# The second parts of the odd attention's queries in tiles of 128 rows, half of them zero

## The chip, the cores and the metric

The kernel runs on one core of one Trainium2 chip. The metric is the device time of one execution in microseconds; the figure of a kernel is the median of its runs. Engines: PE multiplies matrices (PEld is its weight load), DVE, ACT and POOL work on tiles, SP issues most DMAs.

## The reference, cut to what matters

A two-layer encoder runs over a prompt of 512 tokens and a sample of 256 tokens with the same weights, all in float32. Each layer is feed-forward, mixer, feed-forward. The mixer of the second (odd) layer, and the only one that the change touches, is windowed attention with 16 query heads and 4 key heads of 64 features, in blocks of 128 tokens:

```python
s = jnp.einsum('bqgrd,bkgd->bgrqk', q_n, k_n).astype(f32) * scale + bias[None]
s = jnp.where(valid, s, NEG_INF)
m = jnp.maximum(jnp.max(s, axis=-1, keepdims=True), sk)
p = jnp.exp(s - m)
denom = jnp.sum(p, axis=-1, keepdims=True) + jnp.exp(sk - m)
return jnp.einsum('bgrqk,bkgd->bqgrd', (p / denom).astype(v.dtype), v_n)
```

`q_n` holds 128 queries, `k_n` up to 384 keys (the block before, the own block and the block after, as far as the sequence has them).

## The kernel before, in words

Float32 products are made of float32r products: a number x is split into a rounded first part and a second part x - first part, and three of the four products of parts are summed in PSUM. The weights come as tiles `raw`, are split by ACT (first part, L88) and DVE (second part, L89) into tiles `whl`, and are used in a fixed order. `self.look` says how many tiles of weights are prepared ahead. PSUM is a ring of eight banks (`self.ps()`), `raw` a ring of seven tiles.

The six stages run one after the other: ffn 0, `mixer0`, ffn 1, ffn 2, `mixer1`, ffn 3. `mixer1` makes the keys (`keys`, in `kk`), the values (`V`, L1009) and the queries `qT[0]` (`block`, L222), and then weaves two attention passes with dense products: `att(0)` with the four feature blocks of `qT[1]` (L222, emptied by ACT at L893), `att(1)` with half of the output projection (`out_pass`, L389, added to x by DVE at L392). `weave` emits one step of the dense product and then two steps of the attention; the compiler that orders each engine's instructions keeps this nearly as it is, but may mix neighbouring steps.

A pass `att(m)` has 12 units u: six query tiles (order 4, 5, 0, 1, 2, 3) by two key heads (`par`). `queries(t)` splits the queries of a tile: `hh` has the first part of a key head's four query heads twice, above each other (ACT at L927 and L930, POOL at L932), and `lo` has the second parts, par 0 in rows 0 to 63 and par 1 in rows 64 to 127 (DVE, L928). `kk` holds for each key head its first part in the 64 rows that its queries have, and its second part in the other 64. So `scores(u)` needs two matmuls for each of four heads: L956 over all 128 rows gives first part by first part plus first part of the query by second part of the key, and L957, over 64 rows, adds the second part of the query by the first part of the key. DVE adds the bias and takes the maximum (L958), ACT makes the exponentials with their sum (L960), DVE and ACT make the divisor (L962 to L965), DVE scales (L968). `values(u)` transposes the four heads' rows on PE (L978), ACT copies them from PSUM (L981, one copy for each key tile), and for par 1 PE multiplies with the values, 64 output rows for each key head (L990). Then ACT stores (L1017 in `att(0)`, the split at L88 and L89 in `att(1)`).

The order in a step of the weave is: dense step, `values(u)`, `scores(u+2)`, so that a unit's transposes come one dense step, one `values` and one `scores` and another dense step behind its scores. A unit has 256 keys for query tiles 4, 5, 0 and 3, and 384 for tiles 1 and 2.

Of the kernel before, what the change touches and what calls it, by code (L numbers as in the profile page):

```python
# [11 lines left out]
F32 = mybir.dt.float32  # L12
F32R = mybir.dt.float32r
# [6 lines left out]
P = 128  # L20
# [17 lines left out]
# neighbourhood attention: (first query, queries, first key, keys) in the order (column, row)  # L38
NA_Q = [(0, 128, 0, 256), (128, 128, 64, 256), (256, 128, 192, 256), (384, 128, 256, 256),
        (512, 128, 512, 160), (640, 128, 608, 160)]  # L40
# key blocks (first key, keys) of the windows above
# [5 lines left out]
class Trunk:  # L47
# [20 lines left out]
    def warm(self, after):  # L68
        """have the table of the square root loaded as soon as the column "after" is there"""
        w = self.cp.tile([P, 1], F32, tag="warm", name="warm", bufs=2)  # L70
        self.nc.scalar.activation(w, after, AF.Sqrt, bias=self.one, scale=0.0)
# [13 lines left out]
    def split(self, hl, lo, src):  # L85
        """hl (rounded) + lo = src, exactly"""
        nc = self.nc
        nc.scalar.copy(hl, src)  # L88
        nc.vector.tensor_sub(lo, src, hl.bitcast(F32))  # L89

# [6 lines left out]
    def weights(self):  # L97
        """the weights of the whole trunk"""
# [15 lines left out]
        def quad(n, q, b, r1=None):  # L114
            """the parts and sums of two blocks of features; without the head if r1, the first, is given"""
            k = lambda z: (n, q, b, z)
            headed, r1 = r1 is not None, self.raw(self.a[n][q, 2 * b]) if r1 is None else r1
            a11, a12 = r1[:, :512], r1[:, 512:]
            if not headed:
                yield k("11"), self.part(a11)  # L120
            r2 = self.raw(self.a[n][q, 2 * b + 1])
            a21, a22 = r2[:, :512], r2[:, 512:]
            s1 = self.wp.tile([P, 512], F32, tag="st", name="st", bufs=2)
            v.tensor_add(s1, a21, a22)  # L124
            v.tensor_sub(a21, a11, a21)
            v.tensor_sub(a11, s1, a11)
            yield k("s2"), self.part(a11)
            yield k("s1"), self.part(s1)
            if b < 2:
                yield k("22"), self.part(a22)  # L130
            yield k("s3"), self.part(a21)
            if not headed:
                yield k("12"), self.part(a12)
            v.tensor_sub(a12, a12, a11)
            yield k("s4"), self.part(a12)
            if b > 1:
                yield k("22"), self.part(a22)
# [57 lines left out]
    def norm_half(self, t, out):  # L195
        """sum of squares of the first half of token tile t"""
        ss = self.cp.tile([P, 4], F32, tag="ss", name="ss", bufs=6)
        self.nc.scalar.activation(out[:, 0:512], self.x[t][:, 0:512], AF.Square, accum_out=ss[:, 0:1])  # L198
        self.nc.gpsimd.tensor_scalar(ss[:, 1:2], ss[:, 0:1], 1.0 / DM, EPS, ALU.mult, ALU.add)  # L199
        return ss  # L200

    def norm_rows(self, t, gb, out, ss, parts=1):
        """out = rms_norm of token tile t"""
        nc = self.nc
        nc.scalar.activation(out[:, 512:1024], self.x[t][:, 512:1024], AF.Square, accum_out=ss[:, 2:3])
        nc.scalar.activation(ss[:, 3:4], ss[:, 2:3], AF.Sqrt, bias=ss[:, 1:2], scale=1.0 / DM)
        nc.vector.reciprocal(ss[:, 0:1], ss[:, 3:4])
        for e in range(parts):
            c = slice(e * DM // parts, (e + 1) * DM // parts)
            nc.vector.scalar_tensor_tensor(out[:, c], self.x[t][:, c], ss[:, 0:1], gb[:, c], ALU.mult, ALU.mult)  # L210
# [7 lines left out]
    def gemm(self, o, w, act, k0, n, kk=range(KM), last=KM - 1):  # L218
        """o[128 features, n tokens] = w^T act, w stationary; w and act hold four blocks of 128 features to a tile"""
        for k in kk:  # L220
            for j, i in ((0, 0), (0, 1), (1, 0)):
                self.nc.tensor.matmul(o, w[k // 4][:, j, k % 4 * P : (k % 4 + 1) * P], act[i][k // 4][:, k % 4, k0 : k0 + n],  # L222
                                      start=k == 0 and (j, i) == (0, 0), stop=k == last and (j, i) == (1, 0))

    def ffn(self, q, norm, tail, extra=None):
        """gate and up by Winograd's form of Strassen's product over 2 blocks of features, of inputs and of tokens"""
        nc = self.nc
# [3 lines left out]
        with ExitStack() as ctx:  # L231
# [18 lines left out]
            def quad(n, b, use):  # L250
                """steps of the four blocks; use(feature block, token half, value)"""
# [97 lines left out]
    def rows(self, hs, q, b, pos, tail=None):  # L349
        """steps of x += 0.5 h wd over a pair of blocks of features"""  # L350
# [22 lines left out]
    def out_pass(self, name, kb, half, act, tail=None):  # L373
        """steps of x[:, half] += act w over k-block kb (4 of 128 features); act(part, k) has all tokens"""
# [24 lines left out]
    def fgemm(self, f, hn, evac, norm=None, kk=KM):  # L399
        """steps of a feature block of act @ w, feature-major; f names the weights, evac(psum, first token, tokens)"""  # L400
        st = {}

        def part(n, k0, m, ks):
            if not st:
                st["w"] = [self.take(*z) for z in f]
            if ks[0] == 0:
                st["o"] = self.ps()[:, 0:m]
            self.gemm(st["o"], st["w"], hn, k0, m, ks, kk - 1)
            if ks[-1] == kk - 1:
                evac(st["o"], k0, m)  # L410
            if n == 0 and norm:
                norm.finish()

        h = kk // 2
        return [lambda: part(0, NP, NS, range(kk)), lambda: part(1, 0, NP, range(h)), lambda: part(2, 0, NP, range(h, kk))]

# [1 line left out]
    def s5_matrices(self, pool, spare):  # L418
# [10 lines left out]
        class Room:  # L429
            """carves blocks out of tiles"""  # L430
# [26 lines left out]
        def exp(out, x):  # L457
            """exp to float32's accuracy"""
# [51 lines left out]
        # (a - 1) / lambda  # L510
# [15 lines left out]
        # powers 0..8  # L526
# [40 lines left out]
        def start(q):  # L567
            """a pair of groups: W2 (state -> outputs), W1 (inputs -> state)"""
# [28 lines left out]
        def finish(q):  # L597
            """W1 transposed, E (inputs -> outputs)"""
# [44 lines left out]
    def mixer0(self, norm, tail):  # L643
# [4 lines left out]
        with ExitStack() as ctx:  # L648
            mp = ctx.enter_context(self.tc.tile_pool(name="mix0", bufs=1))

            # inputs of S5, in (chunk position, channel) rows
# [14 lines left out]
            def qkv(h):  # L666
                """steps of a head pair's values, queries and keys, in the order (column, row)"""
# [28 lines left out]
            def na(h):  # L696
                """steps of a head pair; q is overwritten by the output, feature-major"""
# [65 lines left out]
            # chunk inputs of the states; both directions run from slot to slot, the reversed one backwards in time  # L763
# [31 lines left out]
            # outputs of S5: chunk inputs through M, states before the chunk through W2  # L795
# [54 lines left out]
            # the neighbourhood half of the output projection around the gate of S5  # L850
# [25 lines left out]
    def mixer1(self, norm, tail):  # L876
        nc, a = self.nc, self.a
        hn = norm.hn
        with ExitStack() as ctx:
# [4 lines left out]
            # a key head's two parts above each other, the first part in the rows that its queries have  # L884
            kk = self.big([P, 4, NT], F32R, name="kk")
            V = mp.tile([P, 6, 256], F32, name="V", tag="V")
            halves = slice(0, 64), slice(64, P)
            pt6, turn = self.big([P, 6, 512], name="pt"), [0]
# [7 lines left out]
            # (query tile, first key tile, key tiles, first column of the bias)  # L896
# [20 lines left out]
            def att(m, store):  # L917
                """steps of the heads of key heads 2m and 2m+1"""
                bias, pend, pts, qq = [] if m else [bias0], {}, [], {}

                def queries(t):
                    """the first parts twice above each other, and the second parts"""
                    q = qT[m][:, :, t * P : (t + 1) * P]
                    hh = self.wp.tile([P, 2, 512], F32R, tag="whl", name="whl", bufs=8).rearrange("p e (h n) -> p e h n", h=4)
                    lo = mp.tile([P, 4, P], F32R, tag="ql", name="ql", bufs=2)
                    for e, r in enumerate(halves):
                        nc.scalar.copy(hh[r, e], q[r])  # L927
                        nc.vector.tensor_sub(lo[r], q[r], hh[r, e].bitcast(F32))  # L928
# [6 lines left out]
                def scores(u):  # L935
# [11 lines left out]
                    r = slice(par * 64, par * 64 + 64)  # L947
                    ps = []
                    hh = (2 * m + par) * 4
                    for h2 in range(2):  # L950
                        p = self.raw()[:, : 2 * 384].rearrange("p (e n) -> p e n", e=2)
                        for e in range(2):
# [4 lines left out]
                            nc.tensor.matmul(s[:, :n], ql[r, h], z[r], start=False, stop=True)  # L957
# [111 lines left out]
def weave(main, *sides):  # L1069
    """emit the steps of main with those of the sides spread between them"""  # L1070
# [13 lines left out]
class NormOut:  # L1084
    """final rms_norm, a token tile at a time"""
# [17 lines left out]
class NormT:  # L1103
    """rms_norm, transposed to feature-major in two parts, a token tile at a time"""
# [41 lines left out]
class NormS(NormT):  # L1146
    """the same as the sums that ffn multiplies with; tokens of tiles 4, 5, 0 and of 1, 2, 3 face each other"""
# [46 lines left out]
    def rest(self):  # L1194
        """the parts that later products take, a step for each"""
# [39 lines left out]
def _na_index(t):  # L1235
    """row of the padded table for each (query, key) of query tile t"""
# [9 lines left out]
def _layout(i):  # L1246
# [13 lines left out]
    # heads of the odd layer: tile (m, r) holds head r of key heads 2m and 2m+1  # L1260
# [5 lines left out]
    # S5  # L1266
# [11 lines left out]
    # biases by constant index; the last entry of the padded table is the masked one  # L1278
# [26 lines left out]
```

## Time and profile before

| | us |
|---|---|
| median of three runs | 2751.83 |
| fastest and slowest run | 2750.31, 2754.99 |
| span of the profiled execution | 2751.6 |
| PE busy in it | 2695.9 (98%) |
| DVE busy | 2008.4 (73%) |
| ACT busy | 1176.3 (43%) |
| POOL busy | 340.6 |

The profiled execution lies within 0.3 us of the median. A matmul's shown duration has a modelled end, and matmuls overlap, so what one costs is read from the distance between the starts of neighbours and not from its duration. A group of weight loads has a count and a total, and where the total is less than count times the single load, loads overlap. In the tables of stretches each engine's field is its busy time in the stretch, PEclk is the granted clock of PE as a share of 2.4 GHz (0.50 is 1.2 GHz).

### The profile page before, as it was taken

The page shows a single profiled execution, that of the slowest core. Times are in us where ns is not written, and L with a number is a line of the kernel's source. Part 1 is how long each engine was busy: PE and PEld are TensorE (multiplying, and loading weights), DVE is VectorE, ACT ScalarE, POOL GpSimd, SP SyncE. Part 2 cuts the span into 40 slices and gives each one's busy share as a digit, 9 for nine tenths or more (in the row PEclk, how much of TensorE's full clock was granted, in tenths as well). Part 3 has the DMA queues.
Part 4 walks back from the last instruction along what each step waited for, and adds up shares of the span by engine and source line. Part 5 has one row for each costly group of instructions (what it writes and reads, how often), then busy time and mean ns, then how long its engine had stood idle before and what let it go on. Part 6 is the DMA issues. An engine that isn't in the chain of part 4 may idle for free.

```text
span 2751.6 us, 38966 instructions
## 1 busy us (share of the span) xinstructions
PE 2695.9 (98%) x14636; PEld 2422.3 (88%) x14636; DVE 2008.4 (73%) x3878; ACT 1176.3 (43%) x2464; POOL 340.6 (12%) x688
## 2 busy tenths in 40 slices
PE   7999999998999999999999999999999999999998
PEld 7988988888888999999989999999876689999997
DVE  8967776772964887677789776767557678777776
ACT  6333333343565633333354333334457664333333
POOL 0156654300840000000000000000000000000000
PEclk9999999999999999999999999999999999999999
DMA  4122222316244222121203121211201123122221
GB/s 155 65 90 85 90 90 77 127 54 134 89 125 142 81 81 85 54 85 54 88 29 122 62 77 62 79 61 39 100 16 39 45 72 108 63 76 68 71 70 54
DMA packets 81245, 217.48 MB, mean 79 GB/s; under 512 B 22848, under 2 KB 29632, under 8 KB 80800
## 3 DMA queue, kind: packets, MB, share of 16 engines
q1 hardware_dynamic: 77152, 203.91, 23.4%
q0 software_dynamic: 3904, 11.08, 1.2%
q8 instruction: 115, 1.88, 0.3%
q14 instruction: 74, 0.61, 0.1%
HBM read 199.17 MB, written 17.89 MB: 79 GB/s over the span
## 4 chain that ended last, share of the span: by engine, by line
PE 92%; DVE 3%; DMA 2%; ACT 2%; POOL 1%; issue 1%; SPq 0%; DVEq 0%; ACTq 0%; POOLq 0%
PE ps L247 44%; PE ps L362 25%; PE ps L222 8%; PE ps L389 5%; PE ps L957 1%; PE ps L990 1%; PE ps L956 1%; PE ps L978 1%; PE ps L1133 1%; PE ps L1009 1%; PE ps L774 1%; PE ps L616 1%; DVE raw L210 1%; PE ps L746 1%; DVE whl L89 0%
## 5 line engine op out<-in xcount | busy, mean ns | idle before, releaser
L88 ACT CAST whl<-raw 128x512 fp32r<-128x512 f32 x796 | 480.3, 621 | 943.7 <-PE ps L362 446.6
L247 PE MATMUL ps<-bt,whl 128*128 128x384 f32 x4224 | 764.6, 336 | 8.9 <-DVE ct L273 8.9
L247 PEld LDWEIGHTS ps<-bt,whl 128*128 128x128 f32 x4224 | 737.9, 189 | 12.5 <-DVE ct L273 10.1
L362 PE MATMUL ps<-whl,hl 128*128 128x512 f32 x3168 | 732.7, 391 | 0.0
L89 DVE TENSOR_TENSOR whl<-raw,whl 128x512 fp32r<-128x512 f32 x796 | 550.6, 705 | 220.2 <-ACT whl L88 209.2
L362 PEld LDWEIGHTS ps<-whl,hl 128*128 128x128 f32 x3168 | 593.9, 188 | 123.5 <-ACT hl L88 0.9
L247 PE MATMUL ps<-b,whl 128*128 128x384 f32 x3168 | 580.3, 336 | 0.0
L247 PEld LDWEIGHTS ps<-b,whl 128*128 128x128 f32 x3168 | 555.1, 189 | 3.5 <-ACT hct L617 0.3
L365 DVE SCALAR_TENSOR_TENSOR x<-ps,x 128x512 f32<-128x512 f32 x528 | 361.5, 689 | 217.5 <-PE ps L362 215.3
L199 POOL TENSOR_SCALAR ss<-ss 128x1 f32<-128x1 f32 x42 | 11.3, 270 | 1787.2 <-ACT raw L198 1787.2
L222 PE MATMUL ps<-hn,whl 128*128 128x256 f32 (+1 forms) x1248 | 231.2, 342 | 1.4 <-ACT hn L88 1.4
L222 PEld LDWEIGHTS ps<-hn,whl 128*128 128x128 f32 x1248 | 191.8, 190 | 31.8 <-issue 3.3
L88 ACT CAST hl<-hct 128x384 fp32r<-128x384 f32 x176 | 86.9, 512 | 50.8 <-DVE hct L317 44.9
L389 PE MATMUL ps<-whl,ob 128*128 128x512 f32 x432 | 105.2, 399 | 0.0
L89 DVE TENSOR_TENSOR hl<-hct,hl 128x384 fp32r<-128x384 f32 x176 | 98.3, 577 | 7.7 <-ACT hl L88 7.4
L389 PEld LDWEIGHTS ps<-whl,ob 128*128 128x128 f32 x432 | 80.7, 190 | 19.7 <-issue 2.2
L279 ACT COPY ct<-ps 128x384 f32<-128x384 f32 x88 | 42.3, 481 | 102.4 <-PE ps L247 102.4
L314 ACT ACTIVATE hct<-ct 128x384 f32<-128x384 f32 x88 | 46.3, 526 | 91.3 <-DVE ct L285 79.9
L284 DVE TENSOR_TENSOR ct<-ps,hct 128x384 f32<-128x384 f32 x88 | 48.9, 556 | 29.3 <-PE ps L247 29.1
L124 DVE TENSOR_TENSOR st<-raw 128x512 f32<-128x512 f32 x88 | 62.6, 712 | 10.1 <-DMA raw<-in_w_gate 9.2
L958 DVE CUSTOM_DVE_ANT_0 raw<-ps,gb,sk 128x256 f32<-128x256 f32 (+1 forms) x96 | 48.6, 525 | 29.0 <-PE ps L957 25.8
L392 DVE TENSOR_TENSOR x<-ps,x 128x512 f32<-128x512 f32 x48 | 33.0, 688 | 48.6 <-PE ps L389 48.6
(235 smaller groups left out, 2632.8 us busy)
## 6 DMA issues: line engine op xcount, KB each, us to landing
raw<-in_w_gate SPq DMA_DIRECT2D x92, 512.0 KB, 3.6
raw<-in_w_up SPq DMA_DIRECT2D x92, 512.0 KB, 3.6
raw<-in_w_down SPq DMA_DIRECT2D x88, 512.0 KB, 3.7
raw<-in_w_in_even SPq DMA_DIRECT2D x16, 512.0 KB, 3.6
raw<-in_w_in_odd SPq DMA_DIRECT2D x10, 512.0 KB, 4.8
W2d<-raw POOLq DMA_DIRECT2D x16, 256.0 KB, 2.4
W1d<-hct POOLq DMA_DIRECT2D x16, 256.0 KB, 3.0
raw<-W1d SPq DMA_DIRECT2D x8, 512.0 KB, 5.5
```

The costliest lines, as they stand in the source:

```text
L88: nc.scalar.copy(hl, src)
L89: nc.vector.tensor_sub(lo, src, hl.bitcast(F32))
L124: v.tensor_add(s1, a21, a22)
L222: self.nc.tensor.matmul(o, w[k // 4][:, j, k % 4 * P : (k % 4 + 1) * P], act[i][k // 4][:, k % 4, k0 : k0 + n], start=k == 0 and (j, i) == ...
L247: nc.tensor.matmul(o, w[:, j, k * P : (k + 1) * P], B[z][:, i, k], start=first and k == 0 and (j, i) == (0, 0), stop=k == 3 and (j, i) == ...
L279: nc.scalar.copy(bank["r5"], bank[3])
L284: v.tensor_add(u3, bank[2], bank["p1"])
L314: nc.scalar.activation(at(f, t), o, AF.Silu)
L362: nc.tensor.matmul(o, h[i][:, pos[t] * P : (pos[t] + 1) * P], w[half][:, j], start=n == 0 and (j, i) == (0, 0), stop=n == len(hs) - 1 and ...
L365: nc.vector.scalar_tensor_tensor(xs, o, 0.5, xs, ALU.mult, ALU.add)
L389: nc.tensor.matmul(o, act(i, k)[:, t * P : (t + 1) * P], st["w"][k][:, j], start=m == 0, stop=m == 11)
L958: nc.vector.tensor_tensor_reduce(p[:, e, :n], s[:, :n], bias[0][:, par * 4 + h, c0 : c0 + n], -1.0, sk[:, 1, hh + h : hh + h + 1], ALU.add ...
```

## The change

The tile `lo` of a query tile, one of two rotating buffers [128, 4, 128], becomes one of two tiles `second[i]` [128, 2, 4, 128] that live as long as `mixer1`. POOL fills both with zeros once at the start of `mixer1`. DVE writes the second parts of key head par to rows `halves[par]` of slot par; the other 64 rows of the slot stay zero. L957 then takes the whole slot and the whole key tile in place of 64 rows of each. The tiles need 4 KB more of each partition, and the reservation for POOL's DMA descriptors is set to 8192 bytes. The full diff also removes comments and docstrings, which moves no line but those below the added ones; they are left out.

```diff
             V = mp.tile([P, 6, 256], F32, name="V", tag="V")
             halves = slice(0, 64), slice(64, P)
+            second = [mp.tile([P, 2, 4, P], F32R, tag=f"ql{i}", name="ql") for i in range(2)]
+            for z in second:
+                nc.gpsimd.memset(z.bitcast(F32), 0.0)
             pt6, turn = self.big([P, 6, 512], name="pt"), [0]
...
-                    lo = mp.tile([P, 4, P], F32R, tag="ql", name="ql", bufs=2)
+                    lo = second[len(qq) % 2]
                     for e, r in enumerate(halves):
                         nc.scalar.copy(hh[r, e], q[r])
-                        nc.vector.tensor_sub(lo[r], q[r], hh[r, e].bitcast(F32))
+                        nc.vector.tensor_sub(lo[r, e], q[r], hh[r, e].bitcast(F32))
...
-                    r = slice(par * 64, par * 64 + 64)
...
                             nc.tensor.matmul(s[:, :n], qh[:, par, h], z, start=True, stop=False)
-                            nc.tensor.matmul(s[:, :n], ql[r, h], z[r], start=False, stop=True)
+                            nc.tensor.matmul(s[:, :n], ql[:, par, h], z, start=False, stop=True)
...
-    nc = _bacc.Bacc("TRN2", target_bir_lowering=False, num_devices=1)
+    nc = _bacc.Bacc("TRN2", target_bir_lowering=False, num_devices=1, dynamic_dma_scratch_size=8192)
```

## Rows read from the trace of the kernel before

**Rows 1.** The page: busy time by engine, share of the span and instructions.
```profile
PE 2695.9 (98%) x14636; PEld 2422.3 (88%) x14636; DVE 2008.4 (73%) x3878; ACT 1176.3 (43%) x2464; POOL 340.6 (12%) x688
```

**Rows 2.** Instructions of PE in order, both passes: start, us, line, operation, shape, count.
```profile
2012.24 0.28 PE L956 MATMUL ps<-kk,whl 128*128 128x256 f32 x1
...
2047.68 0.38 PE L956 MATMUL ps<-kk,whl 128*128 128x256 f32 x1
2047.99 0.38 PE L957 MATMUL ps<-kk,ql 64*128 64x256 f32 x1
...
2050.18 3.06 PE L222 MATMUL ps<-hn,whl 128*128 128x512 f32 x12
...
2053.87 0.42 PE L956 MATMUL ps<-kk,whl 128*128 128x384 f32 x1
...
2056.80 3.14 PE L222 MATMUL ps<-hn,whl 128*128 128x256 f32 x24
2059.77 1.04 PE L978 MATMUL ps<-ident,raw 128*128 128x128 f32 x8
...
2109.59 0.28 PE L956 MATMUL ps<-kk,whl 128*128 128x256 f32 x1
```

**Rows 3.** The same view, whole-array matmuls of 384 columns in a feed-forward.
```profile
1738.72 6.40 PE L247 MATMUL ps<-bt,whl 128*128 128x384 f32 x36
1744.96 4.32 PE L247 MATMUL ps<-b,whl 128*128 128x384 f32 x24
```

**Rows 4.** The same view in the even mixer: score matmuls that all have 64 rows.
```profile
697.90 0.70 PE L710 MATMUL ps<-raw,qT 64*128 64x256 f32 x4
```

**Rows 5.** Weight loads in order: start, us, and idle time of the load path before.
```profile
1958.51 1.61 PEld L1009 LDWEIGHTS ps<-whl,hn 128*128 128x128 f32 x12
...
2054.59 0.19 PEld L956 LDWEIGHTS ps<-kk,whl 128*128 128x128 f32 x1 [0.19 <-issue]
```

**Rows 6.** Groups of PE by shape, 2012 to 2204 us: count, busy us, mean ns.
```profile
L957 PE MATMUL ps<-kk,ql 64*128 64x256 f32 x64 | 25.2, 394 | 0.0
L957 PE MATMUL ps<-kk,ql 64*128 64x384 f32 x32 | 14.0, 437 | 0.0
```

**Rows 7.** Stretches: us, busy PE, PEld, DVE, ACT, POOL (instructions), granted clock, DMA.
```profile
1941.00:1944.00 3.00, 2.60 (x24) 2.37 (x22) 2.96 (x5) 2.48 (x8) 0.00 (x0) 1.00 0.36 137
2015.30:2022.00 6.70, 6.70 (x16) 4.58 (x16) 3.67 (x17) 3.40 (x14) 0.00 (x0) 0.50 0.01 2
2114.20:2117.70 3.50, 3.50 (x9) 2.69 (x9) 2.89 (x13) 3.27 (x9) 0.61 (x1) 0.51 0.00 0
2130.00:2200.00 70.00, 69.62 (x306) 45.48 (x306) 47.27 (x157) 43.15 (x121) 2.90 (x3) 1.00 0.12 39
```

**Rows 8.** The same view: both passes, and the seam between them.
```profile
2012.20:2106.70 94.50, 94.50 (x434) 62.63 (x432) 58.04 (x202) 66.16 (x176) 2.45 (x4) 0.96 0.12 40
2106.70:2204.00 97.30, 96.92 (x411) 62.71 (x410) 68.01 (x219) 61.79 (x169) 4.85 (x6) 0.98 0.13 42
2106.70:2118.90 12.20, 12.20 (x42) 8.57 (x42) 10.10 (x30) 10.16 (x26) 1.95 (x3) 0.86 0.00 0
```

**Rows 9.** Waits in 2012 to 2204 us: us in total, times, longest.
```profile
ACT pt L981 <- PE ps L978: 23.9, 14, 4.9
DVE st L964 <- ACT st L963: 10.3, 17, 1.2
PEld ps L990 <- ACT pt L981: 3.8, 13, 0.8
```

**Rows 10.** POOL in order: a fill, a DMA of its own, its last norm step.
```profile
0.74 0.20 POOL masks.py:197 MEMSET ident<- 128x128 f32 x1 [0.29 <-POOLq L1296]
...
173.87 0.56 POOL L624 DMA_DIRECT2D Ed<-hct  x1 [0.71 <-ACT hct L618]
...
1939.97 0.19 POOL L199 TENSOR_SCALAR ss<-ss 128x1 f32<-128x1 f32 x1 [2.85 <-ACT raw L198]
```

**Rows 11.** DVE in order: the first write of the second parts.
```profile
2007.55 1.71 DVE L928 TENSOR_TENSOR ql<-qT,whl 64x512 fp32r<-64x512 f32 x2 [4.49 <-ACT whl L927]
```

## The prediction

> **What bounds the kernel now.** I read the page first: PE is busy for 98% of the span [rows 1], so time is PE's time, and a change pays only where it makes PE's stream shorter and no other engine then holds PE up. The change touches the two attention passes alone. So next I read PE's instructions in order through them, by the distances between starts. The eight score matmuls of a unit with 256 keys and the step into the dense product take 2050.18 - 2047.68 = 2.50 us, 0.313 us each; with 384 keys 2056.80 - 2053.87 = 2.93 us, 0.366 us each [rows 2], and the pattern repeats in all 24 units. Whole-array matmuls of the same widths, each also with new weights, follow each other much closer: 256 columns 2059.77 - 2056.80 = 2.97 us for 24, 0.124 us each (L222) [rows 2]; 384 columns 6.24 us for 36, 0.173 us each (L247) [rows 3]. So a score matmul costs some 0.19 us more than its columns. The order of the weight loads says what that is: where all matmuls are whole, twelve loads take 1.61 us in all, 0.13 us apart, one beside the stream of another; among the score matmuls each load takes 0.19 us by itself after 0.19 us in which the load path stands idle [rows 5]. Load and stream take turns: 0.19 + 0.18 = 0.37.
>
> What sets these matmuls apart is that their heights alternate, 128, 64, 128, 64. Height 64 alone isn't it: in the even mixer, where all of a run's score matmuls have 64 rows, four of 256 columns take 0.70 us to the end of the last, so at most 0.175 us each, the change into the run included [rows 4].
>
> **The change, part by part.** *Score matmuls.* There are as many as before, with the same columns; the loads have the same 128 columns. The change removes every alternation within a unit, and the one from its last L957 to the dense step. Of L957 there are 64 with 256 keys and 32 with 384 [rows 6], of L956 as many, so 128 and 64 starts. For 256 columns I take the 0.124 us of L222: 128 x (0.313 - 0.124) = 24.2 us. For 384 the 0.173 us of L247: 64 x (0.366 - 0.173) = 12.4 us. Together **36.6 us**, all of it on PE's stream, which doesn't stop in these passes (95 of 95 us and 97 of 97 us busy [rows 8]). After a unit with L990, whose tiles are 64 columns wide, the first load stays alone as now; it is in no distance that I count as gained.
>
> *Clock.* Each pass begins with two units' scores in a row. There the granted clock fell to 0.50, the lower level of 1.2 GHz, for 6.7 us in the first pass and for 3.5 us in the second [rows 7]. Ahead of the falls stood 3.1 and 4.6 us of the alternating pattern without a dense step (2012.24 to 2015.3, 2109.59 to 2114.2) [rows 2, 7]; the other units, of 2.5 to 3 us of it, show no fall (1.00 over 70 us of the second pass [rows 7]). After the change the 16 matmuls go by in about 2.1 us with load beside stream. If the clock stays, PE gets back half of these stretches, 3.4 + 1.7 = **5.1 us**; if it falls all the same, 0. I take 5, because the pattern that stood ahead of both falls is gone.
>
> *What is late next.* PE's two passes would go from 94.5 to about 94.5 - 18.3 - 3.4 = 72.8 us and from 97.3 to 97.3 - 18.3 - 1.7 = 77.3 us. In them ACT has 66.2 and 61.8 us of work, DVE 58.0 and 68.0 us, to which for DVE come some 5 us in each pass in which it waits in order for ACT's exponential of the sums [rows 8, 9]. So ACT will be filled to 91% in the first pass and DVE to 94% in the second, waits included. Neither is the bound on average, but both come near it, and they stand in each other's and PE's chains. Two places by rows. At the seam, 2106.7 to 2118.9, PE's 12.2 us would become 12.2 - 3.0 - 1.7 = 7.5 us, where ACT and DVE have 10.2 and 10.1 us to do (six splits of the first pass's output, queries of two tiles): I take 2.7 us back. Elsewhere the transposes are well covered: between a unit's scores and its transposes lie two dense steps, a `values` and a `scores`, some 8 us even after the change, against some 3 us of softmax. Not covered is ACT's copy between L978 and L990. Now ACT waits 23.9 us for transposes to end, and L990 waits only 3.8 us for copies [rows 9]. With ACT filled up, its copies come behind exponentials and casts of queries that have not yet run, and L990 waits longer. There are 12 `values` with L990; I take 0.6 us for each, 7.2 us. Bounds of the whole item: 0 (ACT and DVE keep ahead, as their sums allow) and half of the gain, 20 us (the pairs of units run at ACT's and DVE's pace with their waits in series). I take **10 us**, nearer to the sums of work than to the chains, since both engines' sums stay under PE's.
>
> *The zeros.* Two fills of 1024 elements a partition: 128 elements took 0.20 us [rows 10], so at most 8 x 0.20 = 1.6 us each. POOL's last norm step is at 1939.97 and the first second part is written at 2007.55 [rows 10, 11]: 67 us of cover, so nothing. If the compiler put both fills ahead of the norm's POOL steps, the norm would be later by at most 3.2 us.
>
> *Descriptor space.* POOL's own DMAs, nearly all ahead of the even mixer, take about 0.56 us each to issue [rows 10]. Nothing in the trace shows POOL waiting for descriptor space, so nothing; the bound is a wait of a few microseconds in all under the first feed-forward, if one such DMA had to wait for the one before. DVE's writes of the second parts have the same 64 x 512 elements, and the two tiles change about as the two buffers did: nothing.
>
> *Sum.* 36.6 + 5.1 - 10 = 31.7 us off the profiled span of 2751.6: 2719.9. The median lies 0.2 us above that span, so **2720 us**.
>
> **The rivals.** *Half of it goes to ACT and DVE.* The mechanism above at its other end: each pair of units waits for its copies and its softmax in series, and the passes shorten by about 19 us instead of 32: 2733. For it speaks that ACT at 91% and DVE at 94% leave almost no room for queues in order; against it, that the slack of a unit is some 8 us and that most of ACT's idle time now is waiting for PE, which shrinks by itself.
>
> *The change doesn't do what it says.* The 0.19 us aren't due to the alternation of heights but to something that stays, such as matmuls whose weights come from tiles that ACT and DVE have only just written; then loads go on taking turns with streams and the time is 2751 or so. Against it: L222 and L247 also take fresh weights and also add into one bank, and run at 0.124 and 0.173 [rows 2, 3]. The Trainium skill speaks for this rival: TensorE: Matmul & The Clock Gate, in Step-by-step: what each phase is for, has PE pull a weight load ahead of running matmuls either where row groups don't conflict or where the load goes to a background buffer. By that rule the 64-row loads of before would be hidden already and the 36.6 us would be 0; the trace doesn't agree, since those loads stand alone with 0.19 us of idle load path before them [rows 5], so I leave this rival a small chance.
>
> *Slower.* PE, now shorter than ACT and DVE at places, stands still in short waits inside every unit, and the granted clock falls there as it did at the two pass starts. A fall like the smaller one costs 1.7 us. One in each of 24 units costs 41 us against 36.6 + 0 gained, and with 10 us of waits the time is 2751.6 - 36.6 + 41 + 10 = 2766. It decides from about 16 falls on (16 x 1.7 + 10 = 37). Against it: where PE stood still for 0.4 us in 3 us, the clock stayed at 1.00 (1941 to 1944) [rows 7], and each unit keeps its dense step.
>
> **How the numbers follow.** My forecast (2709 to 2726, all that lies between no loss and 16 us of it) has 0.62, the half gain 0.24, no effect 0.08, slower 0.06. This kernel's measurement can tell about 0.2%, 5.5 us, from no change. So faster 0.86, same 0.08, slower 0.06. The lower end is the sum without any loss and a little more, 2751.8 - 41.7 = 2710, less 2 us for the spread of runs; the upper is the half gain with 5 us for it: 2708 to 2738, leaving out 0.14.
>
> **What would show it.** Right: L957 in the list of instructions with 128 rows, its starts 0.12 to 0.13 us (256) and 0.17 us (384) after L956's, loads of a unit overlapping, clock 1.00 through both passes, the passes some 75 and 82 us long, ACT and DVE over 80% of them, more wait of L990 for L981. Wrong: distances of 0.31 and 0.37 that stay (the cause is another), clock stretches of 0.50 inside the passes, DVE or ACT ending the waits of L978 or of the scores, or a different length anywhere outside 2007 to 2204 us.

## The result, and the profile after

| | before | after |
|---|---|---|
| median, us | 2751.83 | 2716.52 |
| lowest of the runs, us | 2750.31 | 2712.92 |
| span of the profiled execution, us | 2751.6 | 2713.8 |
| start of the first score matmul, us | 2012.24 | 2012.46 |
| first pass, us | 94.50 | 74.55 |
| second pass, us | 97.28 | 79.17 |

The ratio of the times is 0.987, with an interval of 0.9856 to 0.9885: faster by 32 to 40 us. A fourth run of before lay at 2967.42 us and is left out of the median and the ratio (with it the median is 2753.41). The profiled spans differ by 37.8 us. The two passes, from the first score matmul to the long run of the output projection behind the second, give 38.1 us of it; up to their start the two traces differ by 0.2 us. So the gain is where it was looked for, and all of it.

PE in order after, one unit of each width (as [rows 2]; the lines moved by two, L958 was L956, L959 was L957):

```profile
2037.99 0.39 PE L958 MATMUL ps<-kk,whl 128*128 128x256 f32 x1
2038.21 0.27 PE L959 MATMUL ps<-kk,ql 128*128 128x256 f32 x1
2038.32 0.28 PE L958 MATMUL ps<-kk,whl 128*128 128x256 f32 x1
...
2039.03 2.93 PE L222 MATMUL ps<-hn,whl 128*128 128x512 f32 x12
...
2042.60 0.42 PE L958 MATMUL ps<-kk,whl 128*128 128x384 f32 x1
2042.86 0.34 PE L959 MATMUL ps<-kk,ql 128*128 128x384 f32 x1
2043.03 0.34 PE L958 MATMUL ps<-kk,whl 128*128 128x384 f32 x1
...
2044.08 3.03 PE L222 MATMUL ps<-hn,whl 128*128 128x256 f32 x24
2046.95 1.04 PE L980 MATMUL ps<-ident,raw 128*128 128x128 f32 x8
```

A unit with 256 keys takes 1.04 us (2037.99 to 2039.03) where it took 2.50, one with 384 keys 1.48 us where it took 2.93 [rows 2]. Within a unit starts are 0.12 and 0.175 us apart; only the first distance is longer, 0.20 to 0.28, where transposes or values stand ahead of the unit (behind a dense step it is 0.12). The dense step behind a unit got shorter too: 24 matmuls of 256 columns take 2.87 us (2044.08 to 2046.95) where they took 2.97 [rows 2]. The weight loads of the same unit, with the idle time of the load path where there is any (as [rows 5]):

```profile
2037.99 0.19 PEld L958 LDWEIGHTS ps<-kk,whl 128*128 128x128 f32 x1 [0.81 <-DVE ql L931]
2038.09 0.19 PEld L959 LDWEIGHTS ps<-kk,ql 128*128 128x128 f32 x1
2038.21 0.19 PEld L958 LDWEIGHTS ps<-kk,whl 128*128 128x128 f32 x1
2038.33 0.19 PEld L959 LDWEIGHTS ps<-kk,ql 128*128 128x128 f32 x1
```

A load still takes 0.19 us, but the next begins 0.12 us after it: loads overlap and stand beside the streams. Both passes by engine (us, PE, PEld, DVE, ACT, POOL, granted clock; to [rows 8]):

```profile
2012.46:2087.01 74.55, 74.55 (x434) 57.25 (x433) 55.73 (x202) 63.56 (x176) 2.44 (x4) 1.00 0.15 51
2087.01:2166.18 79.17, 77.38 (x411) 57.02 (x411) 66.22 (x219) 61.17 (x169) 3.93 (x6) 1.00 0.16 52
```

The clock is 1.00 throughout, where it was 0.96 and 0.98. ACT is at 85% of the first pass and DVE at 84% of the second. Waits in the passes (to [rows 9]; L983 was L981, L992 was L990, L966 was L964):

```profile
DVE st L966 <- ACT st L965: 11.2, 16, 1.4
PEld ps L992 <- ACT pt L983: 5.2, 16, 0.8
ACT pt L983 <- PE ps L980: 3.6, 6, 0.8
PE ps L980 <- DVE raw L970: 1.8, 2, 1.4
```

ACT's wait for transposes went from 23.9 to 3.6 us: that was the idle time into which PE could be shortened. What came back is small: 1.4 us more of L992 waiting for copies, 1.4 us more of transposes waiting for DVE at the seam (1.8 against 0.4).

One sign that the prediction gives for being wrong is among these lines, on a small scale: DVE ends waits of L980.

**The account.** It is made from the distances between neighbouring starts of all matmuls of the two passes. From the start of each score matmul to the next start go 64.4 us before and 28.8 us after, 35.7 less. Of this 1.4 us are the clock's (below) and 34.3 us the loads'. Another part of the loads lies behind the units. From the first dense matmul of 512 columns behind a unit to the second it takes 0.335 us before and 0.235 us after, and 0.223 and 0.117 with 256 columns: 0.10 us in each of 23 places, 2.3 us. Together the loads' part is 36.6 us, 0.19 us for each of the 192 changes of height in 24 units.

The clock gave back 4.4 us and not half of the 10.2 us of [rows 7], since score matmuls that take turns with their loads do not take twice as long at 0.50; they start 0.51 us apart there and 0.31 us elsewhere, before:

```profile
2015.78 0.58 PE L957 MATMUL ps<-kk,ql 64*128 64x256 f32 x1
2016.29 0.58 PE L956 MATMUL ps<-kk,whl 128*128 128x256 f32 x1
```

Of the 4.4 us, 1.4 are these matmuls' and 3.0 those of the dense steps behind them (15 in 5.27 us and 12 in 4.21, where the distances outside these stretches add up to 3.58 and 2.88).

So PE gained 34.3 + 2.3 + 4.4 = 41.0 us, and the passes are 38.1 us shorter: 3.0 us went to ACT and DVE. Of these 1.4 us are the wait of the transposes at the seam, and 1.6 us more lie between the starts of the products with the values (L992), whose waits for copies grew by 1.4.

### The profile page after: what moved, and what is told of

The parts are those of the page before. It is cut to its first block, busy times and chain, and to the rows that moved or that the text cites. A ratio compares the mean times of both kernels' runs of the same rounds, so it can differ in the third digit from the quotient of the medians.

```text
span 2713.8 us, 38969 instructions
## 1 busy us (share of the span) xinstructions
PE 2658.7 (98%) x14636; PEld 2413.9 (89%) x14636; DVE 2002.5 (74%) x3878; ACT 1173.3 (43%) x2464; POOL 339.6 (13%) x690
## 4 chain that ended last, share of the span: by engine, by line
PE 90%; DVE 4%; ACT 2%; DMA 1%; POOL 1%; issue 1%; SPq 0%; DVEq 0%; ACTq 0%; POOLq 0%
PE ps L247 44%; PE ps L362 25%; PE ps L222 8%; PE ps L389 5%; PE ps L992 1%; PE ps L980 1%; DVE whl L89 1%; PE ps L1135 1%; PE ps L1011 1%; PE ps L774 1%; DVE x L365 1%; DVE raw L210 1%; PE ps L616 1%; PE ps L811 1%; PE ps L958 1%
## 5 line engine op out<-in xcount | busy, mean ns | idle before, releaser
L88 ACT CAST whl<-st 128x512 fp32r<-128x512 f32 x88 | 54.0, 619 | 29.1 <-PE ps L247 29.1
L125 DVE TENSOR_TENSOR raw<-raw 128x512 f32<-128x512 f32 x88 | 63.8, 725 | 1.9
```

## The experiments

The passes' lengths are read from the traces, since they repeat far better than the time does.

**The changed kernel again**, for that.

> The changed kernel once more, for how far the lengths of the passes repeat: within 0.5 us of 74.55 and 79.17 if nothing in them depends on chance; more where the granted clock falls in one execution and not in another.

Measured: passes of 74.54 and 79.21 us, 2715.5 us in all. Differences of half a microsecond in the passes can be read, by this one repeat, as long as the clock does not fall.

**The reservation alone**, on the kernel before.

```diff
-    nc = _bacc.Bacc("TRN2", target_bir_lowering=False, num_devices=1)
+    nc = _bacc.Bacc("TRN2", target_bir_lowering=False, num_devices=1, dynamic_dma_scratch_size=8192)
```

> The kernel before with nothing changed but the 8192 bytes reserved for POOL's DMA descriptors. Theory (the gain is the score matmuls'): span within 2 us of before's 2751.6, the two attention passes 94.5 and 97.3 us long as before. Rival (the reservation or the shifted addresses move time): a span off by more than 4 us, seen ahead of 1000 us, where POOL's DMAs are.

Measured: one run, 2759.3 us, span 2757.3, passes 96.1 and 98.8 us. Neither of the two as it stands. It gains nothing, so the gain isn't the reservation's. The span is off by as much as the rival said, 5.7 us, of which 2.6 us lie ahead of the passes and 3.1 us in them, but both are the clock's. In the passes (us, busy PE, PEld, DVE, ACT, POOL, granted clock):

```profile
2018.40:2025.40 7.00, 7.00 (x17) 5.02 (x17) 3.21 (x17) 2.76 (x12) 0.00 (x0) 0.51 0.01 2
2117.00:2124.00 7.00, 7.00 (x17) 4.85 (x18) 4.52 (x17) 4.26 (x14) 0.61 (x1) 0.53 0.00 0
```

With a third fall near 2070 there are some 17 us at 0.50 in the passes, where before has 10.2 [rows 7]. Ahead of the passes this trace runs 4.1 us earlier than before's at 800 us, with 6.8 us less at 0.50 up to there, and 2.5 us later at 850. Between them its clock fell and before's did not, first this run, then before:

```profile
826.00:842.00 16.00, 16.00 (x73) 13.59 (x74) 4.23 (x6) 7.01 (x12) 0.00 (x0) 0.57 0.22 74
```

```profile
826.00:842.00 16.00, 15.23 (x111) 12.65 (x111) 6.06 (x11) 9.06 (x16) 0.00 (x0) 1.00 0.59 188
```

Whether the reservation moves such falls stays open. Near 825 us the clock fell in seven of the eight executions with 8192 bytes and in none of the four without; near 220 us it was one and four. In all the clock stood at 0.50 ahead of the passes for 31 to 44 us with 8192 bytes and for 31 to 41 us without, so the time doesn't tell the two apart.

**Grouped by height.** The kernel before, its 64-row tiles kept, in another order.

```diff
+                    z = kk[:, 2 * m + par, kt * P : kt * P + n]
+                    four = [self.ps() for _ in range(4)]
+                    for h, s in enumerate(four):
+                        nc.tensor.matmul(s[:, :n], qh[:, par, h], z, start=True, stop=False)
+                    for h, s in enumerate(four):
+                        nc.tensor.matmul(s[:, :n], ql[r, h], z[r], start=False, stop=True)
```

> The kernel before, 64-row tiles kept, but a unit's four whole-array matmuls first and then its four 64-row ones: two changes of height in a unit in place of eight. Theory (each change of height costs a load that stands alone): 6 of 8 loads come back, 24 x 6 x 0.19 = 27 us, less up to 3 us because DVE starts later in each unit, plus up to 5 us of clock: 2721 to 2729. Rival A (a 64-row load always stands alone): only the three whole-array loads in a row come back, 24 x 3 x 0.19 = 14 us: about 2738. Rival B (loads stand alone for another reason, fresh weights or two matmuls into one bank in turn): no change, 2752.

Measured: 2720.5 us, ratio to before 0.989 (0.9874 to 0.9907); passes 162.3 us together against 191.8, clock 1.00. The theory holds against both rivals. A unit in PE's order (start, us, line, count):

```profile
2030.82 0.71 PE L953 MATMUL ps<-kk,whl 128*128 128x256 f32 x4
2031.46 0.74 PE L955 MATMUL ps<-kk,ql 64*128 64x256 f32 x4
2032.13 3.02 PE L222 MATMUL ps<-hn,whl 128*128 128x512 f32 x12
```

1.31 us in place of 2.50, with matmuls of 64 rows and no zeros. Height 64 costs nothing among its like; the change of height does. What is left over the changed kernel's 1.04 us are two changes, and the single starts of this unit show where each is paid: in the distance before it and in the one behind it. Around the change inside the unit these are 0.21 and 0.22 us in place of 0.12, around the change to the dense step 0.21 in place of 0.12 and 0.335 in place of 0.235. So a change costs 0.19 us, single as in a row. Six of eight changes gone in 24 units are 144 x 0.19 = 27 us; with the clock's 4.4 us that is 2 us more than the 29.5 us by which the passes got shorter.

**All score matmuls over 64 rows.** This leaves out the products of the queries' first parts with the keys' second parts.

```diff
-                            nc.tensor.matmul(s[:, :n], qh[:, par, h], z, start=True, stop=False)
+                            nc.tensor.matmul(s[:, :n], qh[r, par, h], z[r], start=True, stop=False)
```

> The kernel before with all score matmuls over 64 rows: L956 takes the same 64 rows as L957, which leaves out the product of the queries' first part with the keys' second part. Theory (alternation, not height): starts 0.12 and 0.175 us apart within a unit and a change only at its ends, so 8 - 2 loads or more come back: passes about 27 to 38 us shorter together, span 2714 to 2725. Rival A (loads into the half array stand alone, as they go to the same rows that are at work): starts stay at 0.31 and 0.37, span 2750.

Measured: 2718.4 us, span 2716.3, passes 158.9 us, 32.9 less than before.

```profile
2016.13 0.38 PE L956 MATMUL ps<-kk,whl 64*128 64x256 f32 x1
2016.35 0.28 PE L957 MATMUL ps<-kk,ql 64*128 64x256 f32 x1
2016.47 0.28 PE L956 MATMUL ps<-kk,whl 64*128 64x256 f32 x1
...
2017.06 0.28 PE L957 MATMUL ps<-kk,ql 64*128 64x256 f32 x1
2017.27 2.35 PE L222 MATMUL ps<-hn,whl 128*128 128x512 f32 x9
```

Starts 0.12 us apart, and 0.21 at the step into the dense product (2017.06 to 2017.27): here loads into the same 64 rows that are at work hide as well as whole ones do. With the grouped order this settles it: neither height 64 nor fresh weights nor the shared bank, but alternation. The Trainium skill, TensorEngine Tiling (Array Packing), Key Properties, says that a change of tiling mode, and not of the tile alone, drains the engine; the trace agrees, with 0.19 us a start [rows 2, 5] while heights alternate, and 0.19 us for each of the two changes left in a unit of the grouped kernel.

**Where the clock falls.** Three kernels put the alternation, or 16 of it in a row, at different places. The changed kernel with the old form in the first two units of each pass (for the other run, in the third and fourth):

```diff
-                            nc.tensor.matmul(s[:, :n], ql[:, par, h], z, start=False, stop=True)
+                            if u in (0, 1):
+                                r = halves[par]
+                                nc.tensor.matmul(s[:, :n], ql[r, par, h], z[r], start=False, stop=True)
+                            else:
+                                nc.tensor.matmul(s[:, :n], ql[:, par, h], z, start=False, stop=True)
```

> The changed kernel, with L957's old 64-row form in the first two units of each pass alone (16 starts in a row, twice). Theory (alternation without a dense step brings the granted clock down): 32 x 0.194 = 6.2 us for the loads, and two stretches at 0.50 that cost about 5 us: the passes 11 us longer than the changed kernel's 153.7, 165. Rival (the clock fell for something else at the pass starts, as the loading of ACT's table): loads alone, passes 160, or, since DVE and ACT are behind there, less.

Measured: 2721.8 us, passes 77.66 and 83.69, 161.35 us. In the first pass 3.1 us more, 16 changes at 0.19 us and nothing else: the clock stayed at 1.00 over 4.9 us of alternation. In the second pass it fell, and 4.5 us more came out:

```profile
2094.00:2095.00 1.00, 1.00 (x5) 0.59 (x4) 0.98 (x4) 1.00 (x6) 0.00 (x0) 1.00 0.00 0
2095.00:2096.00 1.00, 1.00 (x4) 0.65 (x3) 0.96 (x2) 0.11 (x2) 0.00 (x0) 0.67 0.00 0
2096.00:2097.00 1.00, 1.00 (x3) 0.55 (x4) 0.22 (x2) 0.55 (x2) 0.00 (x0) 0.50 0.00 0
```

Between the two expectations, and neither was right as it stood: the same alternation brought the clock down in one pass and not in the other.

> The changed kernel, with the old form in the third and fourth unit of each pass alone, which have a dense step between them: as many alternations as at the pass starts. Theory: 6.2 us for the loads and no stretch at 0.50: passes 160 us. Rival (any alternation brings the clock down): 165 us with stretches at 0.50 behind both units.

Measured: 2722.7 us, passes 77.48 and 82.10, 159.6 us, clock 1.00 throughout. As the theory had it: 5.9 us for 32 changes and no fall.

The kernel before with the first unit's scores ahead of the first dense step of each pass:

```diff
-            weave([s for f in range(4) for s in block(4 + f, qT[1][:, f], GQ)], att(0, keep))
+            first, *more = att(0, keep)
+            first()
+            weave([s for f in range(4) for s in block(4 + f, qT[1][:, f], GQ)], [lambda: None] + more)
...
```

> The kernel before, with the scores of the first unit of each pass ahead of the first dense step, so that no two units' scores follow each other; nothing else changed, 64-row tiles kept. From the first score matmul to the end of the passes before takes 191.8 us; here the first dense step of 3.0 us lies inside. Theory (16 alternating matmuls in a row bring the clock down, eight don't): clock 1.00 through both passes and 191.8 + 3.0 - 5.1 = 189.7 us. Rival (it is the start of a pass, not the row of 16): stretches at 0.50 as before, 194.8 us.

Measured: 2750.9 us, 190.97 us from the first score matmul to the end of the passes. Both stretches at 0.50 at the starts are gone. But the clock fell once elsewhere, from 2063 to 2067, behind a unit of eight with 384 keys; in the run with the reservation alone the third fall stood at the same unit. So the theory's "eight don't" is wrong. Over all kernels with alternation, the clock fell in or right behind a row of sixteen at 5 of 6 places (before, the reservation alone, the old form at the pass starts), and behind a unit of eight at 2 of 68. In the passes of the other eight executions, of the changed kernel, its repeat, the grouped and the all-64-row kernel and those below, it never fell. So the row's length matters, and where heights don't alternate from matmul to matmul no fall was seen. What decides at a single place these runs don't show.

**Room on ACT: less.** One of the queries' casts on POOL in place of ACT, in the changed kernel.

```diff
-                            nc.scalar.copy(hh[halves[0], 1], q[r])
+                            nc.gpsimd.tensor_copy(hh[halves[0], 1], hh[r, 1].bitcast(F32))
```

> The changed kernel with the fourth cast of the queries (first part of par 1 into rows 0 to 63) on POOL in place of ACT: 12 x 0.62 = 7.4 us less for ACT. Theory (about 4 us of the changed kernel's passes are waits for ACT and DVE, most of them at the seam): 1 to 4 us shorter than the changed kernel, 2713 to 2716. Rival (the waits are DVE's alone, or the cast's longer way through POOL is late): no gain, 2716 to 2719.

Measured: 2715.2 us, ratio to before 0.9874 (0.9853 to 0.9895), the changed kernel's 0.987; passes 75.03 and 80.48, 1.8 us longer. The rival: ACT's 7.4 us less buys nothing in the passes. Of the 1.8 us, 1.1 lie at the seam, where the 16 score matmuls take 2.94 us in place of 1.89 and PE waits 0.7 us among them for DVE's addition to x (L392), which it doesn't in the changed kernel. Whether the cast's way through POOL brought that about isn't shown, so this run alone doesn't say what less work on ACT is worth.

**Room on ACT: more.** A second copy of the transposed rows in units of par 0.

```diff
                         nc.scalar.copy(z, pt)
+                        if par == 0:
+                            nc.scalar.copy(z, pt)
```

> The changed kernel, with ACT's copy of the transposed rows made a second time in the units of par 0, where no product of the values waits for it: 28 x 0.59 = 16.4 us more of ACT, 8.2 in each pass, 72 of 74.6 and 69 of 79.2 us. Forecast's step (waits grow as ACT is filled): 5 us or more. Rival (a unit's slack of some 8 us takes queues in order up, and only the seam counts): under 2.5 us.

Measured: 2721.4 us, passes 157.0 us together, 3.2 more than the changed kernel. Between the two. Of the 15.5 us more of copies a fifth came out on PE, so the slack of a unit takes most of it. It isn't as free as the rival had it either: with ACT busy for 87% of the passes in place of 81%, the wait of the products with the values for copies went from 5.2 to 6.3 us.

**The seam.** The changed kernel with four of the six splits moved on from the seam.

```diff
-            for t in TILES:
-                self.split(*(w[:, :, t * P : (t + 1) * P] for w in ob[0]), qT[0][:, :, t * P : (t + 1) * P])
+            def part0(t):
+                self.split(*(w[:, :, t * P : (t + 1) * P] for w in ob[0]), qT[0][:, :, t * P : (t + 1) * P])
+            for t in TILES[:2]:
+                part0(t)
...
+            def spread(n):
+                dense[n]()
+                if n + 2 < 6:
+                    part0(TILES[n + 2])
...
```

> The changed kernel, with the six splits of the first pass's output (ACT 0.62 us, DVE 0.69 us each), which all stand at the seam, spread over the first dense steps of the second pass: two at the seam, one with each of the next four steps. Theory (what the changed kernel loses to ACT and DVE it loses at the seam, where the transposes wait 1.8 us for DVE): second pass 1 to 2.5 us shorter than 79.2, the wait of the transposes gone; total 2714 to 2716. Rival (the loss is spread over the units, in the copies ahead of L992): second pass within 0.7 us of 79.2.

Measured: 2715.0 us, ratio to before 0.9864 (0.9843 to 0.9884), not to be told from the changed kernel; second pass 78.92 us, 0.25 shorter. The wait stays, first in this kernel, then in the changed one:

```profile
2091.82 2.90 PE L389 MATMUL ps<-whl,ob 128*128 128x512 f32 x12
2096.00 0.44 PE L980 MATMUL ps<-ident,raw 128*128 128x128 f32 x2 [1.28 <-DVE raw L970]
```

```profile
2096.06 0.44 PE L980 MATMUL ps<-ident,raw 128*128 128x128 f32 x2 [1.41 <-DVE raw L970]
```

1.28 us in place of 1.41. The four splits that moved aren't its cause. The rival has the number right and the place wrong, since the wait is still at the seam. What is left there is the softmax of two units in a row with the queries of two tiles ahead of it; that wasn't separated further.

**The values in whole tiles too.** If changes of the rows cost, changes of the columns into and out of L992 might.

```diff
-            V = mp.tile([P, 6, 256], F32, name="V", tag="V")
+            V = mp.tile([P, 6, 2, 2, P], F32, name="V", tag="V")
+            nc.gpsimd.memset(V, 0.0)
...
-                            nc.tensor.matmul(o[e * 64 : e * 64 + 64], V[:, kt + j, kv * 64 : kv * 64 + 64], pts[e][j], start=j == 0, stop=j == nk - 1)
+                            nc.tensor.matmul(o, V[:, kt + j, m, e], pts[e][j], start=(j, e) == (0, 0), stop=(j, e) == (nk - 1, 1))
...
```

> The changed kernel, with the values too in whole tiles: V holds each key head's 64 columns in a tile of 128 with the other 64 zero, and L992 adds both key heads into all 128 rows of PSUM (6144 bytes reserved for descriptors, to make room). Theory (every change of the matmul's shape costs 0.1 to 0.2 us, of columns as of rows): into and out of 12 values 0.28 us each, 3 to 4 us shorter than the changed kernel, passes 150, about 2713. Rival (L992 waits for ACT's copies there anyway): under 1.5 us, passes 152 to 154.

Measured: 2723.0 us, ratio to before 0.9896 (0.9875 to 0.9917); passes 165.5 us, 11.8 longer than the changed kernel's. Neither number came out; the theory isn't tested by it, because another cost covers it. First a group in this kernel, then one of the same 12 in the changed kernel:

```profile
2075.59 5.32 PE L992 MATMUL ps<-pt,V 128*128 128x512 f32 x12
2080.34 0.68 PE L959 MATMUL ps<-kk,whl 128*128 128x256 f32 x1
```

```profile
2153.73 2.80 PE L992 MATMUL ps<-pt,V 128*64 128x512 f32 x12
2156.45 0.39 PE L958 MATMUL ps<-kk,whl 128*128 128x256 f32 x1
```

4.75 us against 2.72, with the same 512 columns streamed by each matmul. The single starts of these two groups say why. In the changed kernel they come in pairs: two starts lie 0.007 us apart, and the next two follow 0.42 to 0.47 us later. In this kernel they come one by one, 0.43 us apart. So in the changed kernel two key heads, which write to the two halves of PSUM's rows, run side by side, and in this one all the matmuls run one after the other. The operands here are float32 and not float32r; a dense float32r matmul of 512 columns takes 0.23 us. The Trainium skill has such a rule in TensorE: Matmul & The Clock Gate, The mechanism (of packing small matmuls): tiles at different positions of the array work at the same time. The paired starts agree with it.

## Why the prediction was right, point by point

The forecast was 2720 us in a range of 2708 to 2738; measured 2716.5. Part of the nearness is luck: the loads come out exactly because two errors cancel, and the one term that was far off, the waits, was the smaller part of the sum.

*What bounds the kernel* was right: the passes got shorter by what PE's stream lost, less 3.0 us, and nothing else moved.

*Loads.* Right in mechanism, as the grouped and the all-64-row kernel show, and in size: 36.6 us measured, 36.6 forecast. But they lie in part elsewhere. The score matmuls gave 34.3 us, because the first start of most units stays at 0.20 to 0.28 us where the sum took 0.124 and 0.173 for all eight. The sum left out the 2.3 us behind the units, where the last change of height also holds up the second dense matmul. The two happen to be equal.

*Clock.* It stayed at 1.00 in both passes, as taken. The reason given holds as far as the runs go: where heights don't alternate from matmul to matmul, no fall came in the passes. That the other units "show no fall" holds for that execution and not for others. The gain was 4.4 us and not 5.1, for the stretches at 0.50 are not twice as long as the same work at 1.00. It is also one execution's: in the run with the reservation alone the clock cost the passes some 3 us more.

*What is late next* is the term that was mis-sized: 10 us taken, 3.0 measured. Both parts were too large. At the seam 2.7 us were expected because ACT and DVE had 10.2 and 10.1 us of work for PE's 7.5; the transposes wait 1.4 us there, and moving four of the six splits that the forecast named didn't help. For the copies ahead of L992 0.6 us a group were expected, 7.2 us; it is 1.6 us. The mistake is to take the share of a filled engine as a price. ACT at 85% of the first pass let its copies come nearly in time; that a unit's transposes stand a dense step and more behind its softmax would explain it, but wasn't tested. The run with more on ACT shows the price of going further, some 0.2 us for each microsecond.

*The zeros and the descriptors.* Right. The compiler did put both fills ahead of the norm's POOL steps, but they ended before the first of those was due (0.95 us each; first norm step at 1923.87, before at 1923.64):

```profile
1918.44 1.85 POOL L890 MEMSET ql<- 128x1024 f32 x2 [485.67 <-DVE hct L317]
1923.87 0.19 POOL L199 TENSOR_SCALAR ss<-ss 128x1 f32<-128x1 f32 x1 [3.57 <-ACT raw L198]
```

*The rivals.* Half the gain lost: not here. No effect: excluded. By the rule of the Trainium skill that the prediction sets beside this rival (TensorE: Matmul & The Clock Gate, Step-by-step), 64-row loads would be hidden already. In the all-64-row kernel they are, with starts 0.12 us apart; in the kernel before, across changes of height, they are not. Slower by falls of the clock: the other way about, the shorter kernel has none in its passes.

*What the tests left.* No version was told from the changed kernel by its time, so none is recommended over it. Open are why the clock falls at one place and not at another with the same alternation, what makes the 1.4 us at the seam, and whether changes of columns cost anything.

## What to carry to other kernels

Read matmuls by the distance between their starts, and hold it against a run of plain ones of the same width: here an excess equal to a weight load went with loads that stood alone, and what alternated was the cause. Look also at the first start behind a changed group: a part of the cost lay there, in rows that the change doesn't touch. Either remedy works, zeros to make all tiles one shape or an order that groups the shapes; here the zeros were worth 38 us in the passes and the order 29 us, without any memory, each with the clock's 4.4 us in it. But a small tile is no waste where its neighbour runs at the same time: filling it up made a group of the values' matmuls take 4.75 in place of 2.72 us.

## What the runs showed of the hardware that was not expected

The granted clock fell in one place and not in another under the same instructions: the kernel before had 10.2 us at 0.50 in its passes in one execution, the same code with another reservation some 17 us, and of two rows of 16 alternating matmuls in one execution one ended at 0.50 and the other at 1.00. PE was busy throughout both rows. At 0.50 alternating score matmuls started 0.51 us apart and not 0.63, so half of such a stretch is too much to count as lost.

A score matmul of 64 rows among its like starts every 0.12 us, as fast as one of 128. The cost is in the change alone: 0.19 us, single as in a row, half of it in the distance before the change and half in the one behind it.

Float32 matmuls of 64 output rows, two key heads for the two halves of PSUM's rows, started in pairs 0.007 us apart; with 128 rows they started one by one, 0.43 us apart.
